# First projection in contraction parts of 2, 4, 5 and 5, with the modulation tiles made between weight pieces

## The chip, the cores and the metric

The kernel runs on one core of a Trainium2 chip. The metric is device time in microseconds (us), the median of several runs; smaller is better. Engines are called by the names of the profile: PE (matmul), PEld (weight load of PE), DVE (VectorE), ACT (ScalarE), POOL, SP (which issues the loads).

## The reference, cut to what matters

Two transformer blocks follow each other on 256 tokens of width 2048, in fp32. Only the start of the first one is touched by the change:

```
mod = silu(c) @ w_ada + b_ada            # c: 2048 numbers; six vectors of 2048
shift1, scale1, gate1, ... = split(mod)
h = rms_norm(x, norm1_w) * (1 + scale1) + shift1
proj = h @ w_in                          # 2048 -> 8192 columns
u, q, k, v, g_a, g_b = split(proj)       # pool input, attention, two gates
```

The first projection needs shift1 and scale1 for all 2048 channels, and these cost a read of 32 MiB of w_ada. Behind it come the pool branch, attention, the output projection, a feed-forward part, and the second block of the same size.

## The kernel before, in words

**Weights.** All large products stream their weights from HBM in blocks of 1 MiB, 128 x 4 x 512 numbers (four tiles of 128 x 512). A block is prepared in two halves: ACT casts a half to fp32r (`hi`, L201), DVE subtracts this from the raw half (`lo`, L209). A tile of weights makes a unit of six matmuls of 512 columns, three for each 128 tokens: x_hi by hi (L303), x_hi by lo (L304), x_lo by hi (L305). So a block is 24 matmuls. There are four raw buffers, four hi and four lo.

**Order.** `run` writes the program half block by half block: it first records the preparation of the halves up to three ahead (LOOK = 3), then the units of the present one, then what a finished segment needs. Each engine executes its instructions in the order in which they were recorded. A segment (`Seg`) is one group of 512 output columns with its range of contraction tiles k; its two PSUM tiles `acc` (one for each 128 tokens) come from four buffers, so two segments are open at a time. `ga0` and `ga1`, two column groups of the gate, sit in the four other PSUM tiles through the whole first projection.

**The ada products.** A vector element group of mod (128 channels) is one load of 1 MiB of w_ada and one DVE multiply-and-sum over 2048 columns (L177), against silu(c) spread over all partitions (`cb`). With products k and 16+k done, `h_tile(k)` makes the modulated activations of contraction tile k: DVE makes two columns of scale and shift (`sAB`, L563, L565), ACT the fp32r half (L384), DVE the full value (L385) and the low half (L386).

**The first projection.** It is 48 blocks. So that PE can begin before all of mod is there, the contraction runs in parts of k: 0 to 3, 4 to 9, 10 to 15 (`CHUNKS`). In a part, all twelve column groups (four of g_a, q, k, u, v by two) are multiplied; the partial sums of ten of them are kept in SBUF. The first part is copied there by ACT (L607), later ones are added by DVE (L609). A table `when` says at which block each further ada product and h tile is made: from block 5 every 1.1 blocks, and from block 19.5 every 1.05. The first four blocks each make their own two products and h tile.

**Loads.** SP issues all loads in the order of one queue: `pump` stops at the first entry, weight block or ada tile, that has no free buffer (four raw, two ada).

**The start.** c is loaded as one row on one partition, silu is taken there, and four matmuls with a row of ones (L497) spread it; DVE copies the result to `cb`. x is scaled by its 1/rms on DVE (L545) and then transposed.

Of the kernel before, what the change touches and what calls it, by code (L numbers as in the profile page):

```python
# [18 lines left out]
P = 128  # L19
# [12 lines left out]
ADAB = 2  # L32

# [12 lines left out]
class Seg:  # L46
# [5 lines left out]
    def __init__(self, lhs, ks, end=None, tag="acc", end_tt=None, tail=2):  # L52
        self.lhs, self.ks, self.end, self.tag, self.end_tt = lhs, list(ks), end, tag, end_tt
        self.tail = tail if end_tt else 0
        self.acc = None
        self.left = [len(self.ks)] * 2

# [6 lines left out]
class Net:  # L64
    def __init__(self, ctx, tc, A):
        self.ctx, self.tc, self.nc, self.A = ctx, tc, tc.nc, A
        mk = lambda name, bufs, **kw: ctx.enter_context(tc.tile_pool(name=name, bufs=bufs, **kw))
        self.fix = mk("fix", 1)
        self.rawp = mk("rawp", RAWB)
        self.hlp = mk("hlp", HLB)  # L70
        self.adap = mk("adap", ADAB)
        self.actp = mk("actp", 4)
        self.t2p = mk("t2p", 4)
        self.psp = mk("psp", 4, space=PSUM)
        self.dramp = mk("dramp", 1, space=bass.MemoryType.DRAM)
# [11 lines left out]
        self.q_dma = 0  # L87
# [69 lines left out]
    def pump(self):  # L157

        while self.q_dma < len(self.queue):
            kind, what, src = self.queue[self.q_dma]  # L160
            if kind == "w":
                if what - self.prepped // 2 >= RAWB:
                    return
                t = self.rawp.tile([P, 4, 512], F32, tag="raw", name="raw")
                self.nc.sync.dma_start(out=t, in_=src)
                self.raw[what] = t
            elif kind == "a":
                if len(self.ada_dma) - self.ada_done >= ADAB:
                    return
                t = self.adap.tile([P, D], F32, tag="ada", name="ada")  # L170
                self.nc.sync.dma_start(out=t, in_=src)
                self.ada_dma.append(t)
            self.q_dma += 1
# [120 lines left out]
    def unit(self, seg, k, hi, lo, tts=(0, 1)):  # L294
        if seg.acc is None:
            seg.acc = [self.psp.tile([P, 512], F32, tag=seg.tag, name="acc") for _ in range(2)]
        for tt in tts:
            first = seg.left[tt] == len(seg.ks)
# [4 lines left out]
            self.nc.tensor.matmul(a, xh, hi, start=first, stop=False)  # L303
            self.nc.tensor.matmul(a, xh, lo, start=False, stop=False)  # L304
            self.nc.tensor.matmul(a, xl, hi, start=False, stop=last)  # L305
# [178 lines left out]
    def setup(self):  # L484
        nc, fix, A = self.nc, self.fix, self.A

        row = self.mixp.tile([1, 2 * D], F32, tag="B", name="crow")
        nc.sync.dma_start(out=row[:, 0:D], in_=A["c"].unsqueeze(0))
        nc.vector.memset(row[:, D:D + P], 1.0)
        self.cb = fix.tile([P, D], F32, tag="cb", name="cb")  # L490
        self.tables("silu")
        nc.scalar.activation(row[:, 0:D], row[:, 0:D], AF.Silu)
        self.tables("exp")
        self.cbps = []
        for i in range(4):
            ps = self.ms()
            nc.tensor.matmul(ps, row[:, D:D + P], row[:, i * 512:(i + 1) * 512], start=True, stop=True)  # L497
            self.cbps.append(ps)
# [5 lines left out]
        self.cst = fix.tile([P, 2, P], F32, tag="cst", name="cst")  # L504
        nc.sync.dma_start(out=self.cst, in_=A["cst"])
        nc.sync.dma_start(out=self.pkt, in_=A["pk"])
        self.mask = self.t2([P, P], name="mask")
        nc.sync.dma_start(out=self.mask, in_=A["mask"])
        self.ident, self.tri = (self.cst[:, i, :] for i in range(2))
# [6 lines left out]
        self.mod2 = fix.tile([P, 96], F32, tag="mod2", name="mod2")  # L516

# [10 lines left out]
    def block1(self):  # L528
# [12 lines left out]
        junk = mp.tile([P, D], F32, tag="u", name="junk")  # L541
        for tt in range(2):
            nc.scalar.activation(junk, x[:, tt, :], AF.Square, accum_out=tot[:, tt:tt + 1])
            r = self.rstd(tot[:, tt:tt + 1], 1, D)
            nc.vector.tensor_scalar(out=x[:, tt, :], in0=x[:, tt, :], scalar1=r, scalar2=None, op0=ALU.mult)  # L545
            if tt == 0:
                for i, ps in enumerate(self.cbps):
                    nc.vector.tensor_copy(self.cb[:, i * 512:(i + 1) * 512], ps)
        nc.vector.scalar_tensor_tensor(out=wb, in0=self.pk("b_ada", 16, 16), scalar=1.0, in1=self.pk("norm1_w"),
                                       op0=ALU.add, op1=ALU.mult)  # L550
        xT = mp.tile([P, KD, S], F32, tag="B", name="xT")

        for tt in range(2):
            for c in range(4):
# [4 lines left out]
        self.at(6, self.setup2)  # L559

        def h_tile(k):
            sAB = self.fix.tile([P, 2], F32, tag="sAB", name="sAB", bufs=2)
            nc.vector.tensor_scalar(out=sAB[:, 0:1], in0=mod[:, 16 + k:17 + k], scalar1=self.pk("norm1_w", k, 1),  # L563
                                    scalar2=wb[:, k:k + 1], op0=ALU.mult, op1=ALU.add)
            nc.vector.tensor_tensor(out=sAB[:, 1:2], in0=mod[:, k:k + 1], in1=self.pk("b_ada", k, 1), op=ALU.add)  # L565
            self.modulate(xT[:, k, :], get(k // 4)[:, k % 4, :, :], sAB[:, 0:1], sAB[:, 1:2])
# [58 lines left out]

        held = {("ga", g): Seg(h_lhs, range(16), lambda acc, g=g: gate_a(g, acc), "ms") for g in range(2)}
        w = A["win1"]
        chunk = {}
# [3 lines left out]
        for c, (b0, every) in enumerate(((5, 1.1), (19.5, 1.05)), 1):  # L632
            for i in range(2 * (ch[c + 1] - ch[c])):
                when.setdefault(int(b0 + every * i), []).append((ch[c] + i // 2, i % 2))
        for nb, bl in enumerate(startup_blocks()):
# [7 lines left out]
            for key, k in bl:  # L643
                c = max(i for i in range(len(ch)) if ch[i] <= k)
                if key not in held and (key, c) not in chunk:
                    chunk[key, c] = Seg(h_lhs, range(ch[c], ch[c + 1]), part_end(key, c))
# [794 lines left out]
CHUNKS = (0, 4, 10, 16)  # L1441


def startup_blocks():
# [4 lines left out]
    for c in range(len(ch) - 1):  # L1449
# [4 lines left out]
        else:  # L1454
            rest = [keys[i] for i in (2, 3, 4, 0, 5, 1, 6, 8, 7, 9, 10, 11)]
# [99 lines left out]
```

## Time and profile before

| | |
|---|---|
| median of 3 runs (lowest, highest) | 2510.93 us (2510.15, 2512.42) |
| the profiled execution | 2512.52 us, its span 2510.7 us |
| PE busy | 2478.9 us, 99% of the span |
| PEld, DVE, ACT busy | 82%, 72%, 50% |
| HBM | 265 GB/s over the span |
| granted TensorE clock, mean | 0.997 |

PE is almost always busy by the page, so the time that a change can give or take is found where PE waits. The views that show it are the busy time of each engine by stretch, the waits of PE, and the timeline of one engine: each row there is a start, a duration, the engine and line, the tiles, the shape, and in brackets the idle time before it and what ended it.

### The profile page before, as it was taken

How to read it: one execution, taken by the hardware profiler on the slowest of the kernel's cores; microseconds unless marked ns; L12 is line 12 of the kernel's file. 1: busy time of each engine (PE TensorE's matmuls, PEld its weight loads, DVE VectorE, ACT ScalarE, POOL GpSimd, SP SyncE). 2: the span in 40 equal slices, each digit the busy share in tenths (PEclk: the TensorE clock that was granted, in tenths of full speed). 3: DMA queues.
4: the chain of work that ended last, by engine and by line, in shares of the span. 5: the costliest groups of instructions: out<-in, count | busy, mean ns of one | idle time of the engine just before them, and what ended most of it. 6: DMA issues, size and time to landing. Idle time of an engine off the chain costs nothing.

```text
span 2510.7 us, 29213 instructions
## 1 busy us (share of the span) xinstructions
PE 2478.9 (99%) x11332; PEld 2047.1 (82%) x11332; DVE 1807.3 (72%) x2122; ACT 1259.9 (50%) x1727; POOL 4.0 (0%) x8
## 2 busy tenths in 40 slices
PE   7999999999999999999999999999999999999999
PEld 5778888887888888888887888888788888888887
DVE  7898888888875777787778878766676655456554
ACT  4536645445545444534446556665554453453443
POOL 0000000000000000000000000000000000000000
PEclk9999999999999999999999999999999999999999
DMA  9988678977887778787776655666567655555553
GB/s 358 369 322 318 243 297 323 394 306 286 303 317 284 303 315 316 287 333 306 294 276 222 249 214 211 221 232 223 212 252 278 259 200 194 208 185 191 193 190 130
DMA packets 93580, 666.24 MB, mean 265 GB/s; under 512 B 10817, under 2 KB 11521, under 8 KB 12929
## 3 DMA queue, kind: packets, MB, share of 16 engines
q1 hardware_dynamic: 93442, 664.38, 69.7%
q8 instruction: 89, 1.46, 0.2%
q14 instruction: 49, 0.40, 0.0%
HBM read 660.11 MB, written 4.23 MB: 265 GB/s over the span
## 4 chain that ended last, share of the span: by engine, by line
PE 88%; DVE 6%; ACT 3%; DMA 1%; issue 1%; SPq 0%; ACTq 0%; DVEq 0%
PE acc L303 28%; PE acc L305 28%; PE acc L304 28%; DVE lo L209 2%; DVE ada L177 2%; PE ms L348 1%; DMA raw<-in_win 1%; ACT hi L201 1%; PE ms L1178 1%; PE ms L855 1%; PE ms L1292 0%; ACT hm L1396 0%; PE ms L1410 0%; DVE res L395 0%; PE ms L762 0%
## 5 line engine op out<-in xcount | busy, mean ns | idle before, releaser
L209 DVE TENSOR_TENSOR lo<-raw,hi 128x1024 fp32r<-128x1024 f32 x848 | 1027.6, 1223 | 594.7 <-ACT hi L201 591.6
L201 ACT CAST hi<-raw 128x1024 fp32r<-128x1024 f32 x848 | 884.7, 1051 | 868.1 <-PE acc L305 825.0
L303 PE MATMUL acc<-hi,act 128*128 128x512 f32 x2208 | 875.5, 396 | 7.6 <-ACT hi L201 6.1
L304 PE MATMUL acc<-lo,act 128*128 128x512 f32 x2208 | 864.3, 391 | 9.8 <-DVE lo L209 9.8
L305 PE MATMUL acc<-hi,act 128*128 128x512 f32 x2208 | 863.1, 391 | 0.0
L304 PEld LDWEIGHTS acc<-lo,act 128*128 128x128 f32 x2208 | 416.3, 189 | 99.7 <-DVE lo L209 17.2
L303 PEld LDWEIGHTS acc<-hi,act 128*128 128x128 f32 x2208 | 416.2, 188 | 94.9 <-ACT hi L201 8.4
L305 PEld LDWEIGHTS acc<-hi,act 128*128 128x128 f32 x2208 | 415.9, 188 | 88.1 <-DVE act L1401 0.7
L177 DVE CUSTOM_DVE_ANT_0 ada<-ada,cb 128x2048 f32<-128x2048 f32 x192 | 438.3, 2284 | 0.5 <-DMA ada<-in_ada 0.5
L303 PE MATMUL acc<-hi,f 128*128 128x512 f32 x1024 | 399.1, 390 | 0.0
L305 PE MATMUL acc<-hi,f 128*128 128x512 f32 x1024 | 398.4, 389 | 0.0
L304 PE MATMUL acc<-lo,f 128*128 128x512 f32 x1024 | 398.4, 389 | 0.0
L305 PEld LDWEIGHTS acc<-hi,f 128*128 128x128 f32 x1024 | 192.2, 188 | 40.1
L304 PEld LDWEIGHTS acc<-lo,f 128*128 128x128 f32 x1024 | 192.2, 188 | 39.9
L303 PEld LDWEIGHTS acc<-hi,f 128*128 128x128 f32 x1024 | 192.2, 188 | 39.1
L384 ACT ACTIVATE act<-xT,sAB 128x256 fp32r<-128x256 f32 x16 | 9.6, 601 | 86.2 <-DVE sAB L565 86.2
L419 ACT ACTIVATE relu<-acc 128x512 f32<-128x512 f32 x64 | 37.7, 590 | 29.0 <-PE acc L305 29.0
L350 DVE TENSOR_TENSOR f<-ms,f 128x512 fp32r<-128x512 f32 x64 | 41.0, 683 | 3.1 <-ACT f L349 3.1
L395 DVE TENSOR_TENSOR res<-acc,gate 128x512 f32<-128x512 f32 x32 | 22.0, 689 | 28.2 <-PE acc L305 28.2
L398 ACT ACTIVATE res<-x 128x512 f32<-128x512 f32 x24 | 15.2, 633 | 52.6 <-DVE x L396 52.6
L420 ACT ACTIVATE relu<-relu 128x512 f32<-128x512 f32 x64 | 40.5, 633 | 2.0
L349 ACT CAST f<-ms 128x512 fp32r<-128x512 f32 x64 | 34.4, 589 | 13.8 <-PE ms L348 13.8
(245 smaller groups left out, 1266.8 us busy)
## 6 DMA issues: line engine op xcount, KB each, us to landing
raw<-in_ff SPq DMA_DIRECT2D x240, 1024.0 KB, 5.6
ada<-in_ada SPq DMA_DIRECT2D x192, 1024.0 KB, 5.8
raw<-in_win SPq DMA_DIRECT2D x120, 1024.0 KB, 6.5
raw<-in_ff1p SPq DMA_DIRECT2D x16, 1024.0 KB, 4.8
raw<-in_wa SPq DMA_DIRECT2D x8, 1024.0 KB, 6.9
raw<-in_wb SPq DMA_DIRECT2D x8, 1024.0 KB, 9.1
raw<-in_wop SPq DMA_DIRECT2D x8, 1024.0 KB, 6.9
raw<-in_wo SPq DMA_DIRECT2D x8, 1024.0 KB, 9.7
```

What stands on the lines that cost most here:

```text
L177: self.nc.vector.tensor_tensor_reduce(out=t, in0=t, in1=cb(), scale=1.0, scalar=0.0, op0=ALU.mult, op1=ALU.add, accum_out=mod[:, j:j + 1])
L201: self.nc.scalar.copy(hi, src)
L209: self.nc.vector.tensor_tensor(out=lo, in0=src, in1=hi.bitcast(F32), op=ALU.subtract)
L303: self.nc.tensor.matmul(a, xh, hi, start=first, stop=False)
L304: self.nc.tensor.matmul(a, xh, lo, start=False, stop=False)
L305: self.nc.tensor.matmul(a, xl, hi, start=False, stop=last)
L348: nc.tensor.transpose(ps[:, i, :], src[:, i * P:(i + 1) * P], self.ident)
L349: nc.scalar.copy(dst[:, :, 0, :], ps)
L350: nc.vector.tensor_tensor(out=dst[:, :, 1, :], in0=ps, in1=dst[:, :, 0, :].bitcast(F32), op=ALU.subtract)
L419: nc.scalar.activation(r, acc[tt], AF.Relu)
L420: nc.scalar.activation(r, r, AF.Square)
L855: mm = lambda *a, **kw: nc.tensor.matmul(*a, skip_group_check=True, **kw)
```

## The change

Contraction parts are 2, 4, 5 and 5 tiles of k; the first two blocks make h tiles 0 and 1, the table `when` places the rest at blocks 2 + 0.9 i, 9.5 + 1.2 i and 21.5 + 1.25 i. From the second part on but the last, a segment doesn't add its result to the partial sum: its PSUM tiles are filled with the partial sum by ACT when the segment two places before it ends (`heir`, `init`), PE accumulates on it, and ACT copies it out again. Only in the last part does DVE add. From k = 2 on, the two columns of scale and shift are made by ACT, and the two DVE steps of an h tile stand after the two `lo` of the block that follows the products. x is transposed as it is; its 1/rms is spread over a tile `rows` by two transpositions and multiplied in the first DVE step. c comes as 16 x 128, is transposed, and its 16 columns are spread by 16 more transpositions. Loads go by their own buffers: a weight block no longer waits behind an ada tile or the other way round, and the first four ada tiles use the buffers of the activations, so that six can be on the way.

```diff
     def pump(self):
...
+        while True:
+            n = len(self.ada_dma)
+            w = ws and self.queue[ws[-1]][1] - self.prepped // 2 < RAWB
+            a = ads and (n < ADAX + ADAB or n - self.ada_done < ADAB)
+            if w and (not a or ws[-1] < ads[-1]):
...
     def prep_lo(self):
...
         self.pump()
+        if self.later:
+            self.later.pop(0)()
...
         if seg.end and not any(seg.left):
             seg.end(seg.acc)
+            if seg.heir:
+                seg.heir.open(self)
...
-        for i in range(4):
-            ps = self.ms()
-            nc.tensor.matmul(ps, row[:, D:D + P], row[:, i * 512:(i + 1) * 512], start=True, stop=True)
...
+                nc.tensor.transpose(ps[:, i, :], col[:, j:j + 1].to_broadcast([P, P]), self.ident)
+            nc.vector.tensor_copy(self.cb[:, 4 * c * P:(4 * c + 4) * P], ps.rearrange("p a b -> p (a b)"))
...
-            nc.vector.tensor_scalar(out=x[:, tt, :], in0=x[:, tt, :], scalar1=r, scalar2=None, op0=ALU.mult)
...
+            def first():
+                h.append(self.t2([P, S], name="hm"))
+                nc.vector.scalar_tensor_tensor(out=h[0], in0=src, scalar=sa, in1=rows, op0=ALU.mult, op1=ALU.mult)
+                nc.scalar.activation(dst[:, 0, :], h[0], AF.Identity, bias=sb)
+            def second():
+                nc.vector.scalar_tensor_tensor(out=dst[:, 1, :], in0=h[0], scalar=sb, in1=dst[:, 0, :].bitcast(F32),
+                                               op0=ALU.add, op1=ALU.subtract)
...
+                nc.scalar.activation(sa, ma, AF.Identity, bias=wb[:, k:k + 1], scale=self.pk("norm1_w", k, 1))
+                nc.scalar.activation(sb, mb, AF.Identity, bias=self.pk("b_ada", k, 1))
+                self.later += [first, second]
...
-                    if c == 0:
+                    if c < len(ch) - 2:
                         nc.scalar.copy(d[:, tt, :], acc[tt])
...
+        def back(key):
+            def init(acc):
+                d = part(key)
+                for tt in range(2):
+                    nc.scalar.copy(acc[tt], d[:, tt, :])
...
-        for c, (b0, every) in enumerate(((5, 1.1), (19.5, 1.05)), 1):
+        for c, (b0, every) in enumerate(((2, 0.9), (9.5, 1.2), (21.5, 1.25)), 1):
...
-CHUNKS = (0, 4, 10, 16)
+CHUNKS = (0, 2, 6, 11, 16)
```

In the order of DVE, one h tile in the middle part of the projection. In the kernel before (ISA is the ada product with its read of the sum, `mod_113` the vector of sums), the whole h tile stands between the second product and the next weight halves:

```order
L177 ISA ada,mod_113<-ada,cb 128x2048
L177 ISA mod_113 128x1
L563 TENSOR_SCALAR sAB<-mod_113,pkt,wb 128x1
L565 TENSOR_TENSOR sAB<-mod_113,pkt 128x1
L385 TENSOR_SCALAR hm<-xT,sAB 128x256
L386 TENSOR_TENSOR act<-hm,act 128x256
L209 TENSOR_TENSOR lo<-raw,hi 128x1024 x4
```

In the changed kernel, DVE at the same kind of place (`rrow` is the spread 1/rms):

```order
L194 ISA ada,mod_130<-ada,cb 128x2048
L194 ISA mod_130 128x1
L226 TENSOR_TENSOR lo<-raw,hi 128x1024
L601 SCALAR_TENSOR_TENSOR hm<-xT,sAB,rrow 128x256
L226 TENSOR_TENSOR lo<-raw,hi 128x1024
L605 SCALAR_TENSOR_TENSOR act<-hm,sAB,act 128x256
```

Four small DVE instructions in a row became two that stand each behind a `lo`; the two `sAB` steps are no longer there.

In the order of ACT, the same stretch. In the kernel before, at the end of the first part and the start of the second (`v` is a partial sum in SBUF), the copies end with the first part, and then ACT has one modulation step for each h tile and else only casts:

```order
L607 COPY v<-acc 128x512 x2
L201 CAST hi<-raw 128x1024 x2
L607 COPY v<-acc 128x512 x2
L201 CAST hi<-raw 128x1024
L384 ACTIVATE act<-xT,sAB 128x256
L201 CAST hi<-raw 128x1024 x6
```

In the changed kernel, ACT in the middle of its second part (`qk` and `u` are the partial sums of q, k and u in SBUF):

```order
L616 ACTIVATE sAB<-mod_130,wb,pkt 128x1
L617 ACTIVATE sAB<-mod_130,pkt 128x1
L218 CAST hi<-raw 128x1024
L602 ACTIVATE act<-hm,sAB 128x256
L659 COPY qk<-acc 128x512 x2
L682 COPY acc<-qk 128x512 x2
L218 CAST hi<-raw 128x1024 x2
L659 COPY qk<-acc 128x512 x2
L682 COPY acc<-u 128x512 x2
```

The two `sAB` steps came to ACT ahead of a cast, the modulation step stands between the casts of the two halves of one block, and copies out of and into `acc` stand between it and the next cast.

## Rows read from the trace of the kernel before

**Rows 1.** Page, part 1: busy time, share of the span, instructions.
```profile
PE 2478.9 (99%) x11332; PEld 2047.1 (82%) x11332; DVE 1807.3 (72%) x2122; ACT 1259.9 (50%) x1727; POOL 4.0 (0%) x8
```

**Rows 2.** Busy time by stretch: stretch, its length, engines, granted clock, DMA, GB/s.
```profile
40.00:50.00 10.00, 8.28 (x27) 6.13 (x28) 8.68 (x11) 3.54 (x5) 0.00 (x0) 0.83 1.00 413
...
400.00:2511.00 2111.00, 2097.26 (x9662) 1738.57 (x9660) 1469.24 (x1704) 1052.59 (x1408) 3.75 (x4) 1.00 0.67 255
```

**Rows 3.** Waits of PE, 0 to 400 us: total, times, longest.
```profile
PE acc L304 <- DVE lo L209: 6.5, 9, 0.8
PE acc L303 <- ACT hi L201: 6.1, 3, 3.1
...
PE acc L303 <- DVE gap L609: 1.1, 1, 1.1
PE acc L303 <- ACT gap L607: 0.4, 1, 0.4
```

**Rows 4.** Timeline of PE: starts of blocks 0, 2, 4, two waits, the first matmul behind the projection.
```profile
21.15 0.79 PE L303 MATMUL acc<-hi,act 128*128 128x512 f32 x1 [3.12 <-ACT hi L201]
...
38.68 0.50 PE L303 MATMUL acc<-hi,act 128*128 128x512 f32 x1 [1.99 <-ACT hi L201]
...
55.23 0.50 PE L303 MATMUL acc<-hi,act 128*128 128x512 f32 x1 [0.41 <-ACT gap L607]
55.57 0.39 PE L304 MATMUL acc<-lo,act 128*128 128x512 f32 x1
...
61.94 0.39 PE L305 MATMUL acc<-hi,act 128*128 128x512 f32 x1
...
100.13 0.50 PE L304 MATMUL acc<-lo,act 128*128 128x512 f32 x1 [0.76 <-DVE lo L209]
...
135.08 0.47 PE L303 MATMUL acc<-hi,act 128*128 128x512 f32 x1 [1.05 <-DVE gap L609]
...
318.99 0.48 PE L303 MATMUL acc<-hi,pT 128*128 128x512 f32 x1
```

**Rows 5.** Timeline of DVE over one h tile and the way to the next.
```profile
60.97 0.08 DVE L177 DVE_READ_ACCUMULATOR2_ANT mod<- 128x1 f32 x1
...
62.10 0.43 DVE L386 TENSOR_TENSOR act<-hm,act 128x256 fp32r<-128x256 f32 x1 [0.22 <-ACT act L384]
63.04 1.23 DVE L209 TENSOR_TENSOR lo<-raw,hi 128x1024 fp32r<-128x1024 f32 x1 [0.52 <-ACT hi L201]
64.95 1.23 DVE L209 TENSOR_TENSOR lo<-raw,hi 128x1024 fp32r<-128x1024 f32 x1 [0.68 <-ACT hi L201]
...
68.30 2.36 DVE L209 TENSOR_TENSOR lo<-raw,hi 128x1024 fp32r<-128x1024 f32 x2
70.58 2.29 DVE L177 CUSTOM_DVE_ANT_0 ada<-ada,cb 128x2048 f32<-128x2048 f32 x1
72.78 0.08 DVE L177 DVE_READ_ACCUMULATOR2_ANT mod<- 128x1 f32 x1
```

**Rows 6.** Timeline of ACT over the same h tile.
```profile
61.47 0.60 ACT L384 ACTIVATE act<-xT,sAB 128x256 fp32r<-128x256 f32 x1 [3.88 <-DVE sAB L565]
61.97 1.04 ACT L201 CAST hi<-raw 128x1024 fp32r<-128x1024 f32 x1
62.91 1.05 ACT L607 COPY qk<-acc 128x512 f32<-128x512 f32 x2
```

**Rows 7.** Timeline of ACT at the start: two small steps of the norm.
```profile
10.40 0.29 ACT L334 ACTIVATE rstd<-sstot,eps 128x1 f32<-128x1 f32 x1
10.73 0.20 ACT L336 ACTIVATE rstd<-rstd 128x1 f32<-128x1 f32 x1
```

**Rows 8.** Timeline of DVE at the start: scaling of x, first ada product.
```profile
13.30 1.29 DVE L545 TENSOR_SCALAR x<-x,rstd 128x2048 f32<-128x2048 f32 x1
...
14.59 2.28 DVE L177 CUSTOM_DVE_ANT_0 ada<-ada,cb 128x2048 f32<-128x2048 f32 x1
```

**Rows 9.** DMA view, 0 to 60 us: rate in 40 slices of 1.5 us.
```profile
GB/s 0 93 393 421 431 384 437 431 426 421 295 44 262 410 415 415 426 169 273 421 410 421 431 158 317 410 311 404 421 415 421 426 426 431 437 410 426 295 333 388
```

More of the change, by code (lines that the diff above doesn't have):

```diff
@@ L32 @@
 ADAB = 2
+ADAX = 4
 _PK = {}
@@ L56, in __init__, with open @@
         self.left = [len(self.ks)] * 2
+        self.init = None
+        self.heir = None
+    def open(self, net):
+        self.acc = [net.psp.tile([P, 512], F32, tag=self.tag, name="acc") for _ in range(2)]
+        if self.init:
+            self.init(self.acc)
 def lag(n):
@@ L86, in __init__ @@
         self.pre_end = []
-        self.q_dma = 0
+        self.loads = None
+        self.later = []
         self.q_use = 0
@@ L157, in pump @@
     def pump(self):
[L159 to L171, printed above, removed]
+        if self.loads is None:
+            self.loads = {kind: [i for i, e in enumerate(self.queue) if e[0] == kind][::-1] for kind in "wa"}
+        ws, ads = self.loads["w"], self.loads["a"]
+        while True:
[3 more added lines that the diff above has]
+            if w and (not a or ws[-1] < ads[-1]):
+                _, b, src = self.queue[ws.pop()]
+                t = self.raw[b] = self.rawp.tile([P, 4, 512], F32, tag="raw", name="raw")
+            elif a:
+                src = self.queue[ads.pop()][2]
+                if n < ADAX:
+                    t = self.actp.tile([P, D], F32, tag="act", name="ada")
+                else:
+                    t = self.adap.tile([P, D], F32, tag="ada", name="ada")
                 self.ada_dma.append(t)
-            self.q_dma += 1
+            else:
+                return
+            self.nc.sync.dma_start(out=t, in_=src)
     def ada_product(self, j, mod, cb):
@@ L295, in unit @@
         if seg.acc is None:
-            seg.acc = [self.psp.tile([P, 512], F32, tag=seg.tag, name="acc") for _ in range(2)]
+            seg.open(self)
         for tt in tts:
-            first = seg.left[tt] == len(seg.ks)
+            first = seg.left[tt] == len(seg.ks) and not seg.init
             seg.left[tt] -= 1
@@ L302, in unit @@
             a = seg.acc[tt]
-            self.nc.tensor.matmul(a, xh, hi, start=first, stop=False)
-            self.nc.tensor.matmul(a, xh, lo, start=False, stop=False)
-            self.nc.tensor.matmul(a, xl, hi, start=False, stop=last)
+            mm = lambda *o, **kw: self.nc.tensor.matmul(a, *o, skip_group_check=bool(seg.init), **kw)
+            mm(xh, hi, start=first, stop=False)
+            mm(xh, lo, start=False, stop=False)
+            mm(xl, hi, start=False, stop=last)
             if last and seg.end_tt:
@@ L516, in setup, with load_mask @@
         self.mod2 = fix.tile([P, 96], F32, tag="mod2", name="mod2")
+    def load_mask(self):
+        self.mask = self.t2([P, P], name="mask")
+        self.nc.sync.dma_start(out=self.mask, in_=self.A["mask"])
     def setup2(self):
@@ L558, in block1 @@
                 nc.scalar.copy(xT[:, 4 * c:4 * c + 4, tt * P:(tt + 1) * P], ps)
-        self.at(6, self.setup2)
+        ps = self.ms([P, 2, P])
+        for tt in range(2):
+            nc.tensor.transpose(ps[:, tt, :], r[tt].to_broadcast([P, P]), self.ident)
+        nc.scalar.copy(rows, ps.rearrange("p a b -> p (a b)"))
+        self.at(4, self.load_mask)
+        self.at(10, self.setup2)
         def h_tile(k):
             sAB = self.fix.tile([P, 2], F32, tag="sAB", name="sAB", bufs=2)
[L563 to L566, printed above, removed]
+            sa, sb = sAB[:, 0:1], sAB[:, 1:2]
+            ma, mb = mod[:, 16 + k:17 + k], mod[:, k:k + 1]
+            src, dst = xT[:, k, :], get(k // 4)[:, k % 4, :, :]
+            h = []
+            def first():
[5 more added lines that the diff above has]
+                                               op0=ALU.add, op1=ALU.subtract)
+            if k < ch[1]:
+                nc.vector.tensor_scalar(out=sa, in0=ma, scalar1=self.pk("norm1_w", k, 1), scalar2=wb[:, k:k + 1],
+                                        op0=ALU.mult, op1=ALU.add)
+                nc.vector.tensor_tensor(out=sb, in0=mb, in1=self.pk("b_ada", k, 1), op=ALU.add)
+                first()
+                second()
+            else:
+                nc.scalar.activation(sa, ma, AF.Identity, bias=wb[:, k:k + 1], scale=self.pk("norm1_w", k, 1))
+                nc.scalar.activation(sb, mb, AF.Identity, bias=self.pk("b_ada", k, 1))
+                self.later += [first, second]
         def need(k):
@@ L645, in block1 @@
                 if key not in held and (key, c) not in chunk:
-                    chunk[key, c] = Seg(h_lhs, range(ch[c], ch[c + 1]), part_end(key, c))
+                    seg = chunk[key, c] = Seg(h_lhs, range(ch[c], ch[c + 1]), part_end(key, c))
+                    order.append(seg)
+                    if 0 < c < len(ch) - 2:
+                        seg.init = back(key)
+                        order[-3].heir = seg
                 units.append((held[key] if key in held else chunk[key, c], k))
@@ L1454, in startup_blocks @@
         else:
-            rest = [keys[i] for i in (2, 3, 4, 0, 5, 1, 6, 8, 7, 9, 10, 11)]
+            out += [(g, k) for k in ks for g in keys[2:4]]
+            rest = [keys[i] for i in (0, 4, 1, 5, 6, 8, 7, 9, 10, 11)]
         out += [(g, k) for g in rest for k in ks]
```

41 lines of the change are left out of this document (22 added, 19 removed).

## The prediction

> **What bounds the kernel now.** I read the page's busy shares first, then the busy time by stretch, the waits of PE, and the timelines of PE, DVE and ACT. PE is busy for 99% of the span [rows 1], and from 400 us on there is hardly a gap (2097 of 2111 us) [rows 2], so what can be won or lost lies in the first projection, and what changes there passes on to the end one for one: nothing behind it waits long enough to swallow it. PE's pace is 28 matmuls in 61.94 - 55.57 = 6.37 us, 0.2275 each [rows 4]; a block of 24 is 5.46 us. PE starts block 0 at 21.15, block 2 at 38.68, block 4 at 55.23 [rows 4]: the first four blocks take 34.1 us for 21.8 us of work. In this stretch each block needs two ada products and an h tile on DVE. From block 4 on PE waits only six more times: five for a `lo`, each 0.76 idle plus 0.25 that the record of the matmul in front is longer than the pace, and once 1.1 for a DVE addition (the end of a segment) [rows 3, 4]. With the 0.4 at block 4 that is about 6.2 us. The first matmul behind the projection starts at 318.99 [rows 4]; this is the time to watch.
>
> That PE hardly waits there is narrow. One h tile and what goes with it takes DVE 72.78 - 60.97 = 11.8 us with four `lo` [rows 5]; the table wants one each 2.2 blocks, 12.0 us of PE. So a change that lengthens this round by a microsecond is seen at once.
>
> **The round of an h tile in the changed kernel.** From rows: a product 2.2 (70.58 to 72.78), a `lo` 1.14 (half of the pair at 68.30 to 70.58) [rows 5], a cast to the `lo` behind it 1.07 (61.97 to 63.04) [rows 5, 6], an ACT modulation step 0.5 (61.47 to 61.97) [rows 6], two copies of 128x512 together 1.0 [rows 6], a DVE step of 128x256 0.43 [rows 5]. The two `sAB` steps on ACT have no row; the nearest are the 128x1 steps of the norm with 0.29 (bias column) and 0.20 [rows 7]. I take 0.5 for both; bounds are 0.2 (they overlap) and 0.6.
>
> Before, DVE went from the second product to the next `lo` in 63.04 - 60.97 = 2.07 us, of which 0.74 were waits for ACT [rows 5], and waited 0.68 once more. After, in the order shown: product; wait for `sAB` on ACT, then for the cast that stands behind it (0.15 + 0.5 + 1.07 = 1.7); `lo`; first step 0.43; now ACT can make its modulation step and only then cast the other half, and DVE's next instruction is that half's `lo`, so DVE waits 0.05 + 0.5 + 1.07 = 1.6; `lo`; second step 0.43. With n `lo` in the round this is 4.4 + 1.7 + 0.43 + 1.6 + 0.43 + 1.14 n = 8.6 + 1.14 n. The DVE work is less than before, the round is longer, because DVE and ACT now wait for each other twice.
>
> The table rounds to whole blocks: h tiles 2 to 15 are complete at blocks 2, 4, 6, 8, 10, 13, 15, 17, 20, 22, 25, 27, 30, 32. Two blocks (n = 4) are 13.1 against 10.9 us of PE; three (n = 6) 15.4 against 16.4. If a copy out of or into `acc` stands between the modulation step and the next cast, add 1.0 for each pair: ACT takes them in order, though PE was done with the segment long ago. Hardly any of this is hidden by preparing three halves ahead: the lead (three halves, 8.2 us of PE) is never built up, and PE also waits for the copy itself, because only two segments have PSUM tiles.
>
> **The sum, start to end of the projection:**
> - Start. x lands 0.4 later behind the constants, but scaling x (1.3 from 13.30 on) and a copy of `cb` in front leave the path: the exponent of the second norm ends at 11.3 instead of 10.9, small DVE steps bring the first product to 12.1 instead of 14.59 [rows 7, 8]. Two products 4.4, `sAB` 0.5, first step 0.43, modulation 0.5, cast 1.07: PE starts at 19.0 instead of 21.15. The c chain is done by about 9 and hidden. Loads: x, the constants, six ada tiles and three weight blocks are 11.4 MiB, at about 420 GB/s [rows 9] some 29 us behind the first 2, before block 2 needs them (34.9): no gain, no loss.
> - Block 1: two `lo`, two products, `sAB`, the steps and the cast again: 28.2 (DVE bound, as before).
> - Block 2 needs no new h tile, but stands behind h tile 2. Two `lo` to 30.5, products to 34.9, `lo` at 36.6, first step, modulation, casts of two halves, and only then the copy of `ga2`, whose PSUM tiles block 2 needs: 41.2 against 38.68.
> - Blocks 2 to 4, one copy pair in the way: 13.1 + 1.0 - 10.9 = 3.2. Block 4 starts at 41.2 + 10.9 + 3.2 = 55.3, before 55.23. The whole gain of the start is spent.
> - Blocks 4 to 6: 3.2 again. To 8 and 10: 2.2 each, and 1.9 where `ga2` hands its tiles over to q behind two casts. To 13: 15.4 + 1.9 - 16.4 = 0.9. To 15 and 17: 13.1 + 1.9 - 10.9 = 4.1 each. Together 18.6.
> - Blocks 17 to 32: six rounds with 30 `lo`, 51.6 + 34.2 = 85.8 against 81.9, so 3.9, and about 1 for copies in the way: 5.
> - Off: the 6.2 of waits that the kernel before has here. The ten segments of the middle part that DVE added to before (20 additions) are in that, and are worth nothing else, since DVE has idle time in the new round.
> - The last part has no h tile; as before no wait.
>
> Net 0.1 + 18.6 + 5 - 6.2 = 17.5. The profiled execution took 2512.5 (span 2510.7 and 1.8 around it), 1.6 above the median of the runs: 2530.0 for a profile like it, 2528.4 for the median. The first matmul behind the projection would start at about 336.5.
>
> **Bounds.** With 0.2 for the `sAB` steps each of 14 rounds is 0.3 shorter, minus 4; with 0.6 plus 1.4. The copies into `acc` (40, 20 pairs) have no row with ACT writing PSUM; the nearest are 0.5 for reading it. If they cost next to nothing, the total falls by about 5 (they count only in the five places where they are in the way); if 0.6 each, plus 1. A spread-multiply step at 0.35 or 0.5 in place of 0.43: minus 2, plus 2. A further loss is the clock: after the waits before block 2 the granted clock was 0.83 over 40 to 50 us [rows 2], part of it at 1.2 GHz; gaps of about 7 and 5 us before blocks 2 and 10 could bring the same for some microseconds, 0 to 4 us, since part hides in the next wait. I take 0. All together: plus 6 to plus 26.
>
> On the copies, the Trainium skill ("ScalarE: Activation LUTs", section "Step-by-step: what each stage is for") says that ScalarE reaches PSUM faster than SBUF, so a copy into `acc` should take less than one out of it. No row here shows such a copy. If the pair took 0.6 instead of 1.0, the sum would be about 2 less, 2526. I stay with the row.
>
> **Rivals.**
> 1. The waits between DVE and ACT are covered, faster. Without them a round with four `lo` is 4.4 + 0.86 + 4.6 = 9.8, under the 10.9 of PE. For it speaks that DVE has fewer instructions and ACT is half idle [rows 1]; against it that the order on both engines is fixed and DVE already waits 0.52 and 0.68 for ACT in the round before [rows 5]. Then only blocks 0 to 2 wait, block 4 starts near 49 instead of 55.2 and the 6.2 go: minus 12, 2498. It decides if the round with four `lo` is under 10.9. Chance 0.12.
> 2. The waits are there but cheaper (copies into `acc` short, `sAB` overlapped, both lower bounds): plus 6 to 12, 2520. Chance 0.2.
> 3. As forecast, and the clock falls at the long gaps: plus 20 to 26, 2533. Chance 0.13.
> 4. The round is about as long as PE needs, so the earlier start and the new waits cancel: within 5 us of before, 2511. The start is worth 2.1 at most, so the rest must balance by chance. Chance 0.1.
>
> **How the numbers follow.** 5 us is 0.2% of the time, about what a measurement of this kernel can tell from no change. Forecast 0.45, rivals 2 and 3 0.33: slower 0.78; rival 4: same 0.1; rival 1: faster 0.12. The range reaches from no change to the clock's worst, 2510 to 2536; the likeliest case by itself is 2522 to 2533.
>
> **What would show it.** Right: first matmul of the projection near 19, block 2 only near 41 and waiting for a copy on ACT; in the waits of PE, copies out of and into `acc` with well over 10 us in total where before it was 0.4; on DVE, an idle 1.5 or more before both `lo` of a block with an h tile, ended by ACT casts; the first matmul behind the projection at 330 or later. Wrong: block 4 before 52, or that first matmul before 319; or PE waiting for loads, which the sum puts at nothing.

## The result and the profile after

| | before | after |
|---|---|---|
| median of the runs, us | 2511.27 (2510.15 to 2512.42, 4 runs) | 2542.34 (2541.63 to 2543.07, 4 runs) |
| ratio | | 1.0121, 95% interval 1.0109 to 1.0133 |
| span of the profiled execution | 2510.7 | 2541.3 |
| first matmul behind the projection | 318.99 | 349.18 |

The forecast was 2528.4, with a range of 2510 to 2536: the direction is right, the size is not, 31 us in place of 17.5, and the time lies above the range. Of the 30.6 us of span, 30.2 are there when the projection ends, so nearly all of them arise in it.

First the waits of PE from 0 to 400 us in after (total, times, longest), beside [rows 3].

```profile
PE acc L322 <- ACT acc L682: 11.2, 6, 4.6
PE acc L322 <- ACT gap L659: 6.2, 1, 6.2
PE acc L322 <- ACT v L659: 4.8, 1, 4.8
PE acc L322 <- ACT hi L218: 4.6, 1, 4.6
PE acc L322 <- DVE lo L226: 4.4, 9, 0.8
PE ms L869 <- DMA wp<-in_wpool: 3.6, 1, 3.6
```

Before, PE waited 0.4 for a copy by ACT; now it waits 22.2 for copies into or out of an accumulator (11.2 + 6.2 + 4.8, the first three rows). The last row is one that no step of the prediction has: the second pool weight.

The timeline of PE in after, in the places of [rows 4]: blocks 0 and 2, two later waits at 69.83 and 101.35, the products of the two pool weights, the first matmul behind the projection.

```profile
19.42 0.49 PE L322 MATMUL acc<-hi,act 128*128 128x512 f32 x1 [4.56 <-ACT hi L218]
...
41.58 0.80 PE L322 MATMUL acc<-hi,act 128*128 128x512 f32 x1 [6.25 <-ACT gap L659]
...
69.83 0.79 PE L322 MATMUL acc<-hi,act 128*128 128x512 f32 x1 [4.80 <-ACT v L659]
...
101.35 0.51 PE L322 MATMUL acc<-hi,act 128*128 128x512 f32 x1 [4.60 <-ACT acc L682]
...
323.80 3.62 PE L869 MATMUL ms<-pl,wp 128*128 128x256 f32 x16
...
340.46 5.38 PE L869 MATMUL ms<-pl,wp 128*128 128x256 f32 x16 [3.60 <-DMA wp<-in_wpool]
...
349.18 0.48 PE L322 MATMUL acc<-hi,pT 128*128 128x512 f32 x1
```

The round of an h tile on DVE in after, beside [rows 5], and below it on ACT, beside [rows 6].

```profile
49.45 0.08 DVE L194 DVE_READ_ACCUMULATOR2_ANT mod<- 128x1 f32 x1
51.11 1.22 DVE L226 TENSOR_TENSOR lo<-raw,hi 128x1024 fp32r<-128x1024 f32 x1 [1.58 <-ACT hi L218]
52.26 0.48 DVE L601 SCALAR_TENSOR_TENSOR hm<-xT,sAB,rrow 128x256 f32<-128x256 f32 x1
55.27 1.23 DVE L226 TENSOR_TENSOR lo<-raw,hi 128x1024 fp32r<-128x1024 f32 x1 [2.54 <-ACT hi L218]
56.41 0.48 DVE L605 SCALAR_TENSOR_TENSOR act<-hm,sAB,act 128x256 fp32r<-128x256 f32 x1
56.81 2.29 DVE L194 CUSTOM_DVE_ANT_0 ada<-ada,cb 128x2048 f32<-128x2048 f32 x1
```

```profile
49.57 0.39 ACT L616 ACTIVATE sAB<-mod,wb,pkt 128x1 f32<-128x1 f32 x1 [1.88 <-DVE mod L194]
49.86 0.28 ACT L617 ACTIVATE sAB<-mod,pkt 128x1 f32<-128x1 f32 x1
50.05 1.03 ACT L218 CAST hi<-raw 128x1024 fp32r<-128x1024 f32 x1
52.83 0.51 ACT L602 ACTIVATE act<-hm,sAB 128x256 fp32r<-128x256 f32 x1 [1.75 <-DVE hm L601]
53.24 1.05 ACT L659 COPY qk<-acc 128x512 f32<-128x512 f32 x2
54.18 1.06 ACT L218 CAST hi<-raw 128x1024 fp32r<-128x1024 f32 x1
```

Read the two together. DVE has its second product at 49.45 and stands 1.58 us, since the cast it wants starts at 50.05. That cast reads only a weight piece, and ACT was idle for 1.88 us ahead of it; it stands behind L616 and L617, and L616 waits for DVE's product. The second idle, 2.54, is the same once more: cast behind a pair of copies behind L602, which waits for DVE. From product to product (42.75 to 56.81) the round takes 14.06; forecast, with a pair of copies in the way, 13.1 + 1.0.

The last part: SP's queue and DVE in after, around the second pool weight, and below them PE and SP in before at the same place.

```profile
329.19 0.33 SPq L190 DMA_DIRECT2D raw<-in_wa  x1
334.24 0.33 SPq L190 DMA_DIRECT2D ada<-in_ada  x1
334.66 0.38 SPq L836 DMA_DIRECT2D wp<-in_wpool  x1
```

```profile
331.92 2.28 DVE L194 CUSTOM_DVE_ANT_0 ada<-ada,cb 128x2048 f32<-128x2048 f32 x1
334.13 0.08 DVE L194 DVE_READ_ACCUMULATOR2_ANT mod<- 128x1 f32 x1
```

```profile
296.45 3.61 PE L806 MATMUL ms<-pl,wp 128*128 128x256 f32 x16
...
300.09 0.33 SPq L773 DMA_DIRECT2D wp<-in_wpool  x1
```

PE was done with the first pool weight at 327.4 (its matmuls are at 323.80, 3.62 long), but the load stands on SP behind an ada load, whose buffer DVE frees at 334.13. Before, SP issued it at 300.09, at once behind matmuls that ended at 300.06.

Last the granted clock (the third number from the end; 1.00 is 2.4 GHz, 0.50 is 1.2 GHz), beside the first line of [rows 2]: four stretches of after, then one that holds a fifth, and below them before.

```profile
40.30:47.15 6.85, 5.57 (x13) 4.43 (x14) 5.85 (x6) 4.26 (x8) 0.00 (x0) 0.50 0.94 361
67.60:74.50 6.90, 4.67 (x11) 3.70 (x12) 4.97 (x5) 5.07 (x9) 0.00 (x0) 0.51 0.51 194
101.80:105.20 3.40, 3.40 (x10) 2.64 (x9) 2.46 (x4) 3.00 (x6) 0.00 (x0) 0.50 0.97 366
135.90:139.30 3.40, 3.40 (x9) 2.62 (x9) 2.67 (x3) 3.40 (x6) 0.00 (x0) 0.50 0.25 31
340.00:360.00 20.00, 19.54 (x82) 16.11 (x83) 14.01 (x18) 8.09 (x12) 0.00 (x0) 0.91 0.58 224
```

```profile
40.00:44.60 4.60, 4.60 (x13) 3.64 (x14) 4.08 (x4) 0.00 (x0) 0.00 (x0) 0.63 0.99 399
```

In four stretches at or behind a wait of PE of 3 us or more the level is 1.2 GHz. A fifth, some 3.4 us, follows the wait for the pool weight: the 16 products behind it take 5.03 us to the next matmul, those of the first pool weight 3.26. From block 2 on, before has only the first of the five, and shorter. In blocks 0 and 1 both kernels have one of about 7 us.

### The profile page after: what moved, and what is told of

It reads as the page before. It is cut to its first block, busy times and chain, and to the rows that moved or that the text cites. A ratio compares the mean times of both kernels' runs of the same rounds, so it can differ in the third digit from the quotient of the medians.

```text
span 2541.3 us, 29255 instructions
## 1 busy us (share of the span) xinstructions
PE 2486.1 (98%) x11343; PEld 2053.4 (81%) x11343; DVE 1788.8 (70%) x2072; ACT 1299.3 (51%) x1834; POOL 4.0 (0%) x8
## 4 chain that ended last, share of the span: by engine, by line
PE 85%; DVE 6%; ACT 5%; issue 3%; DMA 0%; SPq 0%; ACTq 0%; DVEq 0%
PE acc L322 80%; DVE lo L226 2%; DVE ada L194 2%; ACT hi L218 2%; PE ms L370 1%; PE ms L1241 1%; PE ms L918 1%; PE ms L1355 0%; ACT qj L803 0%; ACT hm L1459 0%; ACT acc L682 0%; PE ms L1473 0%; ACT qk L659 0%; DVE hm L601 0%; DMA wp<-in_wpool 0%
## 5 line engine op out<-in xcount | busy, mean ns | idle before, releaser
L322 PE MATMUL acc<-hi,act 128*128 128x512 f32 x4416 | 1409.4, 395 | 28.0 <-ACT acc L682 11.2
L322 PE MATMUL acc<-hi,f 128*128 128x512 f32 x2048 | 634.7, 390 | 0.0
L322 PEld LDWEIGHTS acc<-lo,act 128*128 128x128 f32 x2208 | 418.3, 189 | 100.3 <-DVE lo L226 17.3
L322 PE MATMUL acc<-hi,pT 128*128 128x512 f32 x128 | 42.9, 400 | 0.0
L322 PE MATMUL acc<-hi,oT 128*128 128x512 f32 x128 | 40.7, 392 | 0.0
L406 ACT ACTIVATE act<-ms,shiftc,sA 128x256 fp32r<-128x256 f32 x36 | 20.3, 564 | 39.0 <-DVE hm L407 32.9
L616 ACT ACTIVATE sAB<-mod,wb,pkt 128x1 f32<-128x1 f32 x14 | 5.4, 387 | 56.8 <-DVE mod L194 50.9
L370 PEld LDWEIGHTS ms<-cst,relu 128*128 128x128 f32 x256 | 29.9, 140 | 4.2
```

Source lines behind the costliest of these rows:

```text
L322: mm = lambda *o, **kw: self.nc.tensor.matmul(a, *o, skip_group_check=bool(seg.init), **kw)
L370: nc.tensor.transpose(ps[:, i, :], src[:, i * P:(i + 1) * P], self.ident)
```

## The experiments

Ratios are to before, with their 95% interval. Diffs are against after where nothing else is said. The first four runs, x1, x2, x4 and x7, take parts of the change away.

### h tiles at once: x1_h_at_once

```diff
-            if k < ch[1]:
+            if True:
```

Every h tile is now made as the first two are: the columns on DVE, `first()` and `second()` without delay.

> The changed kernel, but every h tile is made at once behind its two products, with the scale and shift columns on DVE, as its first two h tiles are; parts 2+4+5+5, the filling of PSUM by ACT and the load order stay. Theory (DVE and ACT wait for each other twice in each h tile): DVE goes from the second product to the next lo in about 2.5 us instead of lo after 1.7 and once more 1.6 of idle; a round with four lo is about 11.4 to 12.1 us instead of 13.1 to 15, against 10.9 of PE. Of the about 27 us that PE waits between blocks 2 and 32 some 15 to 20 go: 2522 to 2528. Rival (the copies into and out of PSUM and the hand-over of PSUM tiles cost it, wherever the modulation stands): little goes, 2537 or more.

Measured 2522.70, ratio 1.0045 (1.003 to 1.006): 19.6 of the 31 us are gone. So the way h tiles are made is the main cost; which part of it, this run does not tell.

### The filling of PSUM away: x2_dve_adds

```diff
-                    if c < len(ch) - 2:
+                    if c == 0:
                         nc.scalar.copy(d[:, tt, :], acc[tt])
...
-                    if 0 < c < len(ch) - 2:
+                    if False:
                         seg.init = back(key)
```

> The changed kernel, but the second and third parts are added to the partial sums by DVE as before, with no PSUM tiles filled by ACT; the split modulation stays. Theory (waiting of DVE and ACT for each other): the copies behind the modulation step are gone (1 to 2 us in five rounds), but DVE gets 1.2 us for each segment, 2.4 in a round of two blocks, so the time is about the same or longer: 2538 to 2548. Rival (filling PSUM costs it): most of the loss goes, 2518 to 2525.

Measured 2548.36 (1.0148, 1.0133 to 1.0164). The filling is no cost; it saves 6.0, where the prediction gave the additions spared to DVE no worth beyond the waits of before.

### The start alone: x4_start_alone, x8_start_old_queue

x4 puts back before's parts, table and last order, h tiles at once and DVE's additions; x8 puts back the single queue of loads as well.

```diff
...
-        for c, (b0, every) in enumerate(((2, 0.9), (9.5, 1.2), (21.5, 1.25)), 1):
+        for c, (b0, every) in enumerate(((5, 1.1), (19.5, 1.05)), 1):
...
-CHUNKS = (0, 2, 6, 11, 16)
+CHUNKS = (0, 4, 10, 16)
...
```

> The kernel before with only the new start (c spread by transpositions, 1/rms in a tile of its own, ada tiles in the activations' buffers, loads by own buffers); parts 4+6+6, the old table, h tiles at once, DVE additions, the old order of the last part. Theory: first matmul near 19.4 instead of 21.15; each h tile is 0.4 us longer on DVE than before, since its modulation step now waits for the first DVE step, which eats the gain where DVE is the bound; 2508 to 2513, no change or 2 us faster. Rival (the load order or the start are themselves to blame for part of the 31 us): 2516 or more.

Measured 2518.82 (1.0029, 1.0018 to 1.004): the theory missed. Block 0 starts at 19.19 and block 3 at 49.86, before at 21.15 and 48.05. DVE stood there for an ada tile that SP had issued behind four weight blocks:

```profile
42.77 2.29 DVE L194 CUSTOM_DVE_ANT_0 ada<-ada,cb 128x2048 f32<-128x2048 f32 x1 [3.00 <-DMA ada<-in_ada]
```

> This is the start alone (before's parts of 4+6+6, its table and its last order, h tiles made at once, new spread of c and six ada buffers), which ran at 2518.8, 8 over before, with one thing more put back: loads go out in one strict order again, so that a weight block does not pass an ada tile that stands ahead of it. Theory (those 8 us are the own-buffer order: in the start alone DVE stood 3.00 us at 42.77 for an ada tile issued at 32.90 behind four weight blocks, PE then waited 4.45 for block 3 and ran at half clock after it): 2509 to 2513, no wait over 1.5 us at block 3. Rival (the cost lies in the rest of the start, the 0.4 us longer h tile among it): 2516 or more.

Measured 2514.82 (1.0012, 1.0002 to 1.0021). This lies between theory and rival: the wait at block 3 falls from 4.29 (the expectation has 4.45) to 2.31, and 4.0 of 7.9 us go. So the own-buffer order costs 4 with these parts, and the rest of the start costs 3.3, though its first matmul comes 1.3 earlier than before (19.82); which piece of it costs that was not isolated.

### The second pool weight on another queue: x7_wp_own_queue

```diff
-        self.nc.sync.dma_start(out=self.wp[i], in_=self.A["wpool"][i])
+        (self.nc.gpsimd if i else self.nc.sync).dma_start(out=self.wp[i], in_=self.A["wpool"][i])
```

> The changed kernel, but the second load of the pool's weights is issued by POOL, which has nothing else to do, instead of SP. Theory: in the changed kernel this load stood in SP's order behind an ada load whose buffer DVE freed only at 334.1 us, while PE had been done with the old contents since 327.4; PE then waited 3.6 us for it and ran 3.4 us at the lower clock behind that. Issued by itself it lands in time, 4 to 5.5 us go: 2537 to 2538.5. Rival (the transfer itself is late, the rate of the DMA engines is the limit): less than 1 us goes.

Measured 2535.65 (1.0097, 1.0082 to 1.0112), 6.7 less than after; no wait at L869 is left. The order on SP's queue is the cause of that wait. The gain is above the 4 to 5.5 expected; from the start of block 33 to the end of the projection the two traces differ by 5.5 (105.1 and 99.6), and the rest of the 6.7 is not placed.

### What makes the pool weight late: x5_one_queue, x6_last_order

x5 takes before's single queue of loads, x6 before's order of the last part:

```diff
-            out += [(g, k) for k in ks for g in keys[2:4]]
-            rest = [keys[i] for i in (0, 4, 1, 5, 6, 8, 7, 9, 10, 11)]
+            rest = [keys[i] for i in (2, 3, 4, 0, 5, 1, 6, 8, 7, 9, 10, 11)]
```

> After with loads in one strict order again (the six ada buffers stay). Theory (the cost of the change lies in the split h tiles and the clock; the second pool weight still stands behind an ada load that waits for DVE): 2538 to 2545, a wait of PE for the pool weight still there. Rival (loads by own buffers are a large part of the cost, in the middle and at block 47): 2530 to 2536.

> After with before's order of the last part (no pair of v segments taken together at its head); all else as in after. Theory (the new order puts the second pool weight's need and the products of the ada tiles out of step: in the start alone, which has own-buffer loads and the old order, the wait was 0.8): the wait for the pool weight falls to 1 us or less and block 33 to the first pT matmul takes 98.5 to 101 instead of 105.1, 2535 to 2539. Rival (own buffers put the weight behind an ada load whatever the order): the wait stays over 3, 2541 or more.

x5 took 2544.59 (1.0128, 1.0113 to 1.0143), x6 2542.86 (1.0123, 1.0108 to 1.0139); PE still waits 6.2 and 3.3 us for the weight. So neither loads by own buffers nor the last order alone brings it. Every run here with parts of 2+4+5+5 and the weight on SP has this wait (3.3 to 6.2), none with 4+6+6 more than 0.6. What in the new parts puts the product late was not isolated.

### The opening of an accumulator: x10_heir_after

From the order I took it that v waits at 69.83 because ga's new accumulator, opened a segment early, had taken the free PSUM tile.

```diff
             if seg.heir:
-                seg.heir.open(self)
+                if seg.heir.prev.acc is None:
+                    seg.heir.prev.then = seg.heir
+                else:
+                    seg.heir.open(self)
```

> After with one change: where a part's accumulator would be opened and filled while the segment just before it in the order has not been opened, it is opened right behind that one. That is so at one place, ga of part 2 against v1 of part 1 (blocks 4 to 6). Theory (v1 waited 4.96 us for a copy-out of the same moment because the early-opened heir had taken the free PSUM tile): the wait falls to 3.1 or less and the half clock behind it may go, 2536 to 2540.5. Rival (ScalarE's queue is what is late there, whatever tile v1 has): less than 1 us gained, 2541.4 to 2543.

Measured 2543.11 (1.0123, 1.0108 to 1.0139): the wait for v falls to 3.2, one a segment earlier grows from 1.2 to 2.3, and the time stays. This cause falls.

### Which part of the split h tile: x11_sab_dve, x15_cols_behind_cast

x11 leaves the two modulation steps between the weight pieces and puts only the columns (L616, L617) back on DVE:

```diff
-                nc.scalar.activation(sa, ma, AF.Identity, bias=wb[:, k:k + 1], scale=...)
-                nc.scalar.activation(sb, mb, AF.Identity, bias=self.pk("b_ada", k, 1))
+                nc.vector.tensor_scalar(out=sa, in0=ma, ...)
+                nc.vector.tensor_tensor(out=sb, in0=mb, ...)
```

> After with the two column instructions of an h tile (the scale and the bias, 0.39 and 0.28 us on ScalarE) put back on VectorE for all tiles, while its two modulation steps stay between the weight pieces. Theory (what costs is the splitting: each of the two pieces lo starts only when ScalarE's cast behind the modulation step is done, 1.6 to 2.5 us of VectorE idle a tile): VectorE's two idles stay at 1 us or more each and the time at 2535 to 2542. Rival (the two column instructions in front of the cast make the idles): 2522 to 2530.

Measured 2523.92 (1.0052, 1.0038 to 1.0066). My theory, that the split with its two handovers costs, is refuted: with the split kept, 18.4 of x1's 19.6 are gone. x15 keeps both instructions on ACT and moves them behind the cast:

```diff
         self.nc.scalar.copy(hi, src)
+        while self.behind:
+            self.behind.pop(0)()
...
+                self.behind.append(cols)
```

`cols()` is the two `nc.scalar.activation`.

> After with the two column instructions of an h tile still on ScalarE, but one place later: behind the cast of the next weight piece in place of in front of it. Theory (ScalarE works in order, so the cast, which needs nothing of the h tile, waited for VectorE's product by way of the two columns in front of it, and VectorE's next piece lo waited 1.58 for that cast): the idle of 1.58 a tile goes, 2518 to 2526. Rival (ScalarE is late for the h tile whatever the order, and only VectorE's doing the columns helps): 2532 or more.

Measured 2522.43 (1.0042, 1.0028 to 1.0056): 19.9 less with the same instructions on the same engines. The same round on ACT and DVE in x15:

```profile
44.54 1.06 ACT L219 CAST hi<-raw 128x1024 fp32r<-128x1024 f32 x1
49.28 0.39 ACT L620 ACTIVATE sAB<-mod,wb,pkt 128x1 f32<-128x1 f32 x1 [3.68 <-DVE mod L195]
```

```profile
49.16 0.08 DVE L195 DVE_READ_ACCUMULATOR2_ANT mod<- 128x1 f32 x1
49.16 1.22 DVE L229 TENSOR_TENSOR lo<-raw,hi 128x1024 fp32r<-128x1024 f32 x1
50.30 0.48 DVE L604 SCALAR_TENSOR_TENSOR hm<-xT,sAB,rrow 128x256 f32<-128x256 f32 x1
53.32 1.23 DVE L229 TENSOR_TENSOR lo<-raw,hi 128x1024 fp32r<-128x1024 f32 x1 [2.54 <-ACT hi L219]
```

The cast is done 3.6 us before DVE wants it, and `lo` starts with the product's end. The first idle is gone; the second, 2.54, is as it was, and what it costs now is not shown: x1, which has no split, took 2522.70, the same, but there DVE waits 9.2 us in other places, for ACT's modulation steps. DVE's waits for casts up to 350 us, after and x15:

```profile
DVE lo L226 <- ACT hi L218: 77.3, 46, 3.6
```

```profile
DVE lo L229 <- ACT hi L219: 56.1, 35, 3.6
```

21.2 less there, 19.9 less in the time (23.1 between these two profiled executions). Part of it is the clock: in x15 the waits of PE before blocks 10 and 15 are 1.3 each in place of 4.6 and 3.1, and the level stays at 2.4 GHz behind them.

### The repairs together: x16_cols_wp_heir

> After with three repairs together: column instructions behind the cast, the second pool weight on GpSimd's queue, and the accumulator's opening behind its forerunner's. Theory (they are costs in different places): x15's time less 6 to 9, 2510 to 2519. Rival (with one gone the others' places were hidden): within 4 of x15.

Measured 2516.26 (1.0021, 1.0012 to 1.003), 6.2 below x15. The columns (19.9) and the pool weight (6.7) add up: 26.1 of their sum of 26.6 are gone. x9, h tiles at once with the pool weight on GpSimd's queue, came to 2517.24, in the 2514.5 to 2518 expected of it.

### Is a part of the change worth having? x12, x13, x14, x17, x18

These start from before. x12 has only the new spread of c; x13 also fills the middle part's accumulators; x14 adds x10's repair.

> Before with the new spread of c alone (load of 16 rows, one small transpose, 16 transposes of broadcast columns, four copies by VectorE). Theory (block 0 starts 1 to 1.7 us earlier, but the next ada tiles and the clock decide when blocks 1 to 4 start, so most is given back): 2509.5 to 2511.5. Rival (the gain of block 0 carries through): 2508.5 to 2509.5; the other rival, that it costs: 2512 or more.

> As the run before it (before with the new spread of c) and with the middle part's accumulators filled from the stored partial sums, so that VectorE's adds of the middle part become copies of ScalarE. Theory (VectorE is what PE waits for in blocks 12 to 30, 6.5 us in 9 waits, and ScalarE has room there): 1 to 5 us faster than before, 2505.5 to 2510. Rival (the copies stand ahead of casts on ScalarE and cost as much, or an early-opened accumulator takes a PSUM tile): 2511 or more.

x12: 2510.81 (0.9998, 0.9989 to 1.0007), no change: block 0 starts 0.6 earlier, block 2 0.5 later. x13: 2512.62 (1.0008, 0.9999 to 1.0017): the theory missed, by one wait of 5.4 us at block 11, and so did x14.

> Before with the new spread of c and the filling of the middle part (2512.6), with the repair that an accumulator is not opened and filled before the segment ahead of it has its own. Theory (the one wait of 5.4 us at block 11 and the half clock behind it are that early opening; blocks 13 to 33 had shorter waits than before): 2505 to 2509, faster than before. Rival (v1 waits there for something else, or the wait moves to where the accumulator is filled now): 2511 to 2514.

x14: 2513.22 (1.001, 1.0001 to 1.0019); the wait of 5.5 is still there. The rows of ACT in x13 tell why:

```profile
95.65 0.60 ACT L396 ACTIVATE act<-xT,sAB 128x256 fp32r<-128x256 f32 x1 [5.16 <-DVE sAB L578]
96.15 1.03 ACT L210 CAST hi<-raw 128x1024 fp32r<-128x1024 f32 x1
97.09 1.06 ACT L620 COPY v<-acc 128x512 f32<-128x512 f32 x2
```

PE had finished v's segment at 92, but its copy stands behind an h tile that waits for DVE's product. So x17 makes each later h tile behind the matmuls of the half block in hand, and x18 does that in before alone:

```diff
+            while self.post:
+                self.post.pop(0)()
             s += m
...
-                    self.add_call(lambda k=k: h_tile(k))
+                    self.add_call(lambda k=k: self.post.append(lambda: h_tile(k)))
```

The `while` stands in `run`, behind the `unit` calls.

> Before with the new spread of c and the filling of the middle part (2512.6, with one wait of PE of 5.5 us at block 11), now with each h tile of the later parts made behind the products of the half block in hand, so that its ScalarE instruction stands behind the cast and behind the copies out of an accumulator. Theory (ScalarE stood 5.2 us for VectorE's product with the copy of v behind it): the wait at block 11 falls under 2, 2505 to 2509.5. Rival (the wait is the copy's own, or later h tiles are waited for in its place): 2511 or more.

> Before with only that: h tiles of the later parts made behind the products of the half block in hand. Theory (before's waits for lo and hi after block 4, some 7 us, are partly ScalarE standing for an h tile with a cast behind it): 2506 to 2510. Rival (VectorE's own work is the bound there): 2510.5 to 2512.5.

x17: 2506.53, ratio 0.9981 (0.9972 to 0.999). x18: 2508.43, 0.9989 (0.998 to 0.9997). Both theories hold, and x17 is faster than both kernels, before by 4.9 us. It is 1.9 under x18, but their intervals overlap, so what the filling and the new spread of c add to the order is not shown. ACT in x17 at that place, and PE by stretch:

```profile
93.37 1.07 ACT L623 COPY v<-acc 128x512 f32<-128x512 f32 x2
94.32 1.13 ACT L646 COPY acc<-gap 128x512 f32<-128x512 f32 x2
95.36 0.61 ACT L399 ACTIVATE act<-xT,sAB 128x256 fp32r<-128x256 f32 x1
```

```profile
110.00:345.00 235.00, 235.00 (x1072) 195.12 (x1071) 192.88 (x229) 142.17 (x241) 0.00 (x0) 1.00 0.79 307
```

The copy has gone ahead of the h tile, the wait of PE at block 11 is 1.1, and from 110 us to 345 PE has no gap.

## Why the prediction was right about the direction and wrong about the size

Block starts are counted from the matmuls, 24 a block; the forecast's are those of its sum, and the last row has what before took there. The last column is what the stretch took beyond the forecast. The forecasts add up to 335.5, not to the 336.5 of the prediction: it took off 6.2 for before's waits, where before's block starts show 7.1 between blocks 4 and 32 (159.94 us for 28 blocks of 5.46). The 6.2 is five times 1.01 and the 1.1; with the 0.4 at block 4, which the prediction says is in it, the rows give 6.6.

| stretch | forecast, us | measured | off by |
|---|---|---|---|
| to block 2 | 41.2 | 41.6 | 0.4 |
| blocks 2 to 4 | 14.1 | 15.1 | 1.0 |
| 4 to 6 | 14.1 | 18.1 | 4.0 |
| 6 to 10 | 28.1 | 26.5 | -1.6 |
| 10 to 13 | 17.3 | 18.7 | 1.4 |
| 13 to 17 | 30.0 | 30.2 | 0.2 |
| 17 to 32 | 86.9 | 87.3 | 0.4 |
| 32 to the end of the projection | 103.8 | 111.7 | 7.9 |

- **Right:** the start (19.0 forecast, 19.42), its loss by block 2, and the round of an h tile with both its idles (1.7 and 1.6, measured 1.58 and, with copies between, 2.54). The pair of copies that was priced at 1.0 takes 1.05 out of PSUM and 1.12 into it. From block 6 to 32 the sum is 0.4 off in 163 us; so near is luck, since 1.6 less in 6 to 10 stands against 1.4 more in 10 to 13, where the clock, put at 0, took part. Rival 1, a round under 10.9, falls: it is 14.06.
- **The step that failed first:** "The last part has no h tile; as before no wait." It has waits, and by the trace 7.9 us went there. Some 5.5 are the pool weight's: 3.60 of wait and 1.8 because the 16 products behind it ran at 1.2 GHz; x7 shows the cause. 1.2 went in block 32, where PE still waits for a `lo`, and 1.2 in the rest, where waits of 0.6 and 0.2 stand near 304. The prediction counted the loads of the start; it did not follow the second pool weight through SP's order, behind which product it would stand.
- **The step that failed next:** the clock, of which it said "I take 0". Of the matmuls of 512 columns, 40 start in the first four stretches at 1.2 GHz; before has 8 in the one it has there. Each takes 0.2 more (0.43 in place of 0.23), so an estimate is 6.4 at most. The 1.6 at 135.9 do not show in the table, where 13 to 17 is 0.2 off. Blocks 2 to 4 and 10 to 13 show 2.4, and 4 to 6 about 2; the rest there is v's wait of 4.80, where 3.2 stood in the sum. No run holds the clock fixed, so this share is worked out and not shown by an edit. Rival 3, the forecast with the clock falling, came nearest with 2533; what it lacked is the last part's 7.9.
- **Mis-sized, without harm to the sum:** DVE's additions "worth nothing else" are worth 6 (x2). The forecast needed no term for this, because its new rounds were counted without additions.
- **Right, but read too coarsely:** "DVE and ACT now wait for each other twice" put both idles down to the split. x11 and x15 show that the first one carries 18 to 20 us of the loss, and x1, with no split at all, is no faster than x15. A round without the first is 12.4 in x15 (54.86 to 67.25), and the table's three-block rounds (16.4 of PE) have room for that.

Of the 31 us, 19.9 (x15) and 6.7 (x7) are settled by one edit each. About 5 are left in x16; with before's parts the start costs 3.3 without the own-buffer loads (x8), but how the 5 are split between start, parts and load order in after stays open.

## What to carry to other kernels

On an engine that works in order, an instruction that waits for another engine delays everything behind it, so put work that does not need that engine (casts, copies that free an accumulator) ahead of it: here the order alone, with the same instructions, was worth 20 us in after (x15) and 3 in before (x18, where DVE's steps of the h tile moved as well). When a change lengthens or shortens a stretch, follow each later load through its queue's order too, since one that stands behind a load with a buffer still in use starts when that buffer comes free. Small waits that return in each round can count for more than what a change saves once at the start: here 1.58 us in a round against 1.7 at the first matmul.

## What the runs showed of the hardware

- A copy of 128x512 by ACT takes about as long into an accumulator as out of one, 604 and 588 ns. By line and shape in after (count, busy, mean ns):

```profile
L659 ACT COPY qk<-acc 128x512 f32<-128x512 f32 x24 | 13.0, 588 | 3.7 <-PE acc L322 3.6
...
L682 ACT COPY acc<-qk 128x512 f32<-128x512 f32 x16 | 9.0, 604 | 0.0
...
L652 ACT ACTIVATE m<-gap 128x512 f32<-128x512 f32 x4 | 2.4, 633 | 0.6 <-DVE gap L661 0.6
...
L652 ACT ACTIVATE m<-acc 128x512 f32<-128x512 f32 x4 | 2.2, 593 | 0.0
```

  The Trainium skill ("ScalarE: Activation LUTs", section "Step-by-step: what each stage is for") says that ScalarE reaches PSUM faster than SBUF, and means where it writes. The two copies do not test that, since they differ in what they read as well. For reading, the sigmoid (L652) took 593 ns from PSUM and 633 from SBUF; no run here has the same step write into both.
- ACT and DVE never passed a waiting instruction in these rows. ACT was idle for 1.88 us before 49.57 with a cast behind it that x15 ran at 44.54, and DVE's `hm` stood behind `lo` until 52.26, though its columns were done at 50.14. The Trainium skill ("Perfetto Trace Analysis", section "Tensor Engine Instruction (MATMUL, LD_WEIGHTS)") calls both strict FIFO, and the trace agrees.
- In after the clock fell at or behind waits of PE of 6.25, 4.80, 4.60, 3.60 and 3.08 us and not after one of 2.30 (before 150.25). But in before it fell at 41.3, behind waits of 1.99 and 0.76, and in x15 at 52.6, behind one of 2.45. So the length of the last wait does not decide it; what does, these runs do not tell.
